# Summing 32768 rows of float32: loads without a cast, one running float32 sum on VectorE, TensorE for the last rows only

## The chip, the cores and the metric

The kernel runs on one core of a Trainium2 chip; the other cores are idle. The metric is the device time of one execution in microseconds (us); lower is better.

## The reference

```python
def setup_inputs():
    batch, seq, dim = 32, 1024, 2048
    return {"grad_output": np.random.randn(batch, seq, dim).astype(np.float32)}

def reference(grad_output):
    return np.sum(grad_output, axis=(0, 1)).astype(np.float32)
```

There are 32768 rows of 2048 numbers, 268.4 MB, to be read, and 8 KB to be written. In this text "a row" of work is a block of 128 rows, one per partition (1.05 MB in memory). There are 256 of them.

## The kernel before

The input is loaded in tiles of eight such rows, 8.39 MB each. The requests are issued by GpSimd, and the transfer casts to float16 on the way. VectorE adds the two halves of a tile, which leaves 8192 columns, and TensorE multiplies these with a column of ones, which sums over the partitions. The sums of all tiles accumulate in four PSUM banks.

```python
PRE_TILES = 2                 # two float32 rows first, on the sync queue
BULK_M = 8
BULK_TAPER = (4, 2)
TAIL_TILES = 5                # five single rows, then one row in four column pieces
T_BUFS = 3
TAIL_BUFS = 8
BULK_ENGS = ("gpsimd",)
# ... [plan: 2 float32 rows; 30 tiles of 8; 2, 4, 2, 1,1,1,1,1 rows; 4 pieces] ...

    for i, entry in enumerate(plan):
        # ... [T is a float16 tile from one of the pools] ...
        getattr(nc, eng_name).dma_start(out=T[:], in_=src)
        red = T
        if uses_dve(entry):
            half = (m * col_n) // 2
            C = c_pool.tile([P, half], fp16, tag="C", name=f"c{i}")
            nc.vector.tensor_tensor(out=C[:], in0=T[:, :half], in1=T[:, half:],
                                    op=mybir.AluOpType.add)
            red = C
        w = ones16 if dt_ is fp16 else ones32        # [128, 1] of ones
        for j in range(n_chunks(entry)):
            nc.tensor.matmul(accs[b][:, :], lhsT=w[:],
                             rhs=red[:, j * MM_N : (j + 1) * MM_N],
                             start=(not started[b]), stop=(n_mm[b] == total_mm[b]))
    # ... [four copies out of PSUM, two on ScalarE and two on VectorE; one store] ...
```

## Time and profile before

| | before |
|---|---|
| median time | 629.0 us (628.98 to 629.04, 3 runs) |
| span of the profiled run | 627.2 us |
| memory read | 268.4 MB, 428 GB/s over the span |
| busy: TensorE, VectorE | 31%, 22% |
| share of the 16 DMA engines used by GpSimd's queue | 98.9% |

The page of the kernel before begins with the busy time of each engine. The row called DMA gives the busy tenths of the 16 DMA engines in 40 slices of the span. The line of a queue (q0 is GpSimd's, q1 the sync queue's) gives its packets, the MB that it wrote (half of those read, because of the cast) and its share of the engines.

```profile
PE 195.1 (31%) x536; PEld 58.1 (9%) x536; DVE 138.9 (22%) x37; ACT 2.4 (0%) x3; POOL 22.6 (4%) x46
...
DMA  9999999999999999999999999999999999999997
...
q0 software_dynamic: 6048, 133.17, 98.9%
q1 hardware_dynamic: 290, 2.11, 0.9%
...
HBM read 268.44 MB, written 0.01 MB: 428 GB/s over the span
```

Nothing but the transfers is busy throughout. The next lines are VectorE's timeline: start, duration, what it did, and in brackets how long it was idle before and what ended the wait.

```profile
27.41 4.42 DVE L152 TENSOR_TENSOR c<-t 128x8192 f16<-128x8192 f16 x1 [26.51 <-DMA t<-in_grad_output_dram]
46.74 4.43 DVE L152 TENSOR_TENSOR c<-t 128x8192 f16<-128x8192 f16 x1 [14.90 <-DMA t<-in_grad_output_dram]
66.06 4.43 DVE L152 TENSOR_TENSOR c<-t 128x8192 f16<-128x8192 f16 x1 [14.90 <-DMA t<-in_grad_output_dram]
...
588.89 4.42 DVE L152 TENSOR_TENSOR c<-t 128x8192 f16<-128x8192 f16 x1 [14.94 <-DMA t<-in_grad_output_dram]
```

The additions start 19.3 us apart, although one takes only 4.4 us, and each waits for a transfer. A tile of 8.39 MB in 19.32 us is 434 GB/s of reading. What an engine does inside these 19.3 us costs nothing as long as it fits.

The end of the span, on all engines:

```profile
620.52 3.57 PE L161 MATMUL psum<-t,ones 128*1 128x512 f16 x8 [0.96 <-DMA t<-in_grad_output_dram]
...
622.85 0.57 ACT L175 COPY res<-psum 1x512 f32<-1x512 f32 x1 [620.82 <-PE psum L161]
...
624.13 0.68 DVE L177 COPY res<-psum 1x512 f32<-1x512 f32 x1 [0.17 <-PE psum L161]
624.90 0.32 SPq L178 DMA_DIRECT2D out_dram<-res  x1
```

At 620.52 us the last single row has arrived and TensorE starts eight matmuls without a gap. Four belong to this row and four to the last row, which comes in four pieces.

### The profile page before, as it was taken

The numbers are of one execution on the slowest core, as the hardware profiler recorded it, in microseconds if no ns is written. First come the engines' busy times: TensorE is split into PE (matmuls) and PEld (weight loads), VectorE is DVE, ScalarE is ACT, GpSimd is POOL, SyncE is SP. The second block draws the span as 40 slices with busy tenths as digits, with TensorE's granted clock in tenths as the row PEclk, the third lists the DMA queues.
The fourth block names the chain that finished last, engine by engine and source line by source line (L and its number), as shares of the span: only waits on it lengthen the run. The fifth ranks groups of instructions, "written<-read, shape, count | busy, mean of one in ns | idle before, by whom it ended". The sixth has DMA issues, their size and how long they took to land.

```text
span 627.2 us, 1267 instructions
## 1 busy us (share of the span) xinstructions
PE 195.1 (31%) x536; PEld 58.1 (9%) x536; DVE 138.9 (22%) x37; ACT 2.4 (0%) x3; POOL 22.6 (4%) x46
## 2 busy tenths in 40 slices
PE   3323320333203333123341134321333312343165
PEld 0001100011000111001110011100111000111011
DVE  0202222022220122211222202222022221122320
ACT  0000000000000000000000000000000000000000
POOL 1000000000000000000000000000000000000110
PEclk9677556775567665667655776656676567665677
DMA  9999999999999999999999999999999999999997
GB/s 242 226 234 201 234 201 234 202 232 203 232 203 232 203 232 203 232 204 230 205 230 205 230 205 230 205 230 206 228 207 228 207 224 211 224 211 221 206 206 139
DMA packets 6344, 135.36 MB, mean 216 GB/s; under 512 B 705, under 2 KB 1217, under 8 KB 1857
## 3 DMA queue, kind: packets, MB, share of 16 engines
q0 software_dynamic: 6048, 133.17, 98.9%
q1 hardware_dynamic: 290, 2.11, 0.9%
q8 instruction: 4, 0.07, 0.0%
q14 instruction: 2, 0.02, 0.0%
HBM read 268.44 MB, written 0.01 MB: 428 GB/s over the span
## 4 chain that ended last, share of the span: by engine, by line
another core or an unknown queue 66%; DVE 21%; DMA 11%; PE 1%; POOL 1%; issue 0%; DVEq 0%; POOLq 0%
DVE c L152 20%; DMA t<-in_grad_output_dram 11%; PE psum L161 1%; POOL t L146 1%; DVEq L152 0%; DVE res L177 0%; POOLq L193 0%
## 5 line engine op out<-in xcount | busy, mean ns | idle before, releaser
L161 PE MATMUL psum<-c,ones 128*1 128x512 f16 x496 | 175.9, 533 | 405.5 <-DVE c L152 405.5
L152 DVE TENSOR_TENSOR c<-t 128x8192 f16<-128x8192 f16 (+2 forms) x33 | 137.5, 4167 | 471.1 <-DMA t<-in_grad_output_dram 471.1
L161 PEld LDWEIGHTS <-ones 128*1 128x1 f16 x520 | 56.5, 109 | 537.5 <-issue 516.4
L146 POOL DMA_DIRECT2D t<-in_grad_output_dram x42 | 22.4, 538 | 590.4 <-DVE c L152 575.3
L161 PE MATMUL psum<-t,ones 128*1 128x512 f16 (+1 forms) x40 | 19.4, 639 | 23.5 <-DMA t<-in_grad_output_dram 23.5
L177 DVE COPY res<-psum 1x512 f32<-1x512 f32 x2 | 1.4, 679 | 13.9 <-PE psum L161 13.9
L161 PEld LDWEIGHTS psum<-t,ones 128*1 128x1 f32 x16 | 1.6, 106 | 27.5 <-DMA t<-in_grad_output_dram 14.1
L175 ACT COPY res<-psum 1x512 f32<-1x512 f32 x2 | 1.1, 575 | 621.1 <-PE psum L161 621.1
L175 ACT ACT_TABLE_LOAD x1 | 1.3, 1283 | 0.7 <-PEq L193 0.7
L104 DVE MEMSET ones<- 128x1 f16 x1 | 0.1, 59 | 0.8 <-PEq L193 0.8
L193 POOL MEMSET const-float32-0.0<- 128x1 f32 x1 | 0.1, 100 | 0.2 <-issue 0.2
L193 POOL MEMSET const-bfloat16-1.0<- 128x1 bf16 x1 | 0.1, 103 | 0.0
L193 POOL MEMSET const-float32-1.0<- 128x1 f32 x1 | 0.1, 100 | 0.0
L193 POOL MEMSET const-uint8-127<- 128x1 uint8 x1 | 0.1, 100 | 0.0
L108 DVE MEMSET ones<- 128x1 f32 x1 | 0.1, 59 | 0.0
## 6 DMA issues: line engine op xcount, KB each, us to landing
t<-in_grad_output_dram POOLq DMA_DIRECT2D x30, 4096.0 KB, 53.1
t<-in_grad_output_dram POOLq DMA_DIRECT2D x5, 512.0 KB, 20.4
t<-in_grad_output_dram SPq DMA_DIRECT2D x2, 1024.0 KB, 14.3
t<-in_grad_output_dram POOLq DMA_DIRECT2D x2, 1024.0 KB, 26.6
t<-in_grad_output_dram POOLq DMA_DIRECT2D x1, 2048.0 KB, 29.0
t<-in_grad_output_dram POOLq DMA_DIRECT2D x4, 128.0 KB, 16.1
out_dram<-res SPq DMA_DIRECT2D x1, 8.0 KB
```

Source lines behind the costliest of these rows:

```text
L104: nc.vector.memset(ones16[:], 1.0)
L108: nc.vector.memset(ones32[:], 1.0)
L146: getattr(nc, eng_name).dma_start(out=T[:], in_=src)
L152: nc.vector.tensor_tensor(out=C[:], in0=T[:, :half], in1=T[:, half:], op=mybir.AluOpType.add)
L161: nc.tensor.matmul(accs[b][:, :], lhsT=w[:], rhs=red[:, j * MM_N : (j + 1) * MM_N], start=(not started[b]), stop=(n_mm[b] == total_mm[b]),)
L175: nc.scalar.copy(out=dst, in_=accs[b][:, :])
L177: nc.vector.tensor_copy(out=dst, in_=accs[b][:, :])
L193: nc = _bacc.Bacc("TRN2", target_bir_lowering=False, num_devices=1)
```

## The change

The intent is to drop the cast, to let the sync queue issue the loads, to keep one float32 sum of 128x2048 on VectorE in place of pair sums in float16, and to use TensorE only for the last rows. There it works in four column groups, each with 32 columns of ones and its own quarter of the partitions of PSUM. The diff, cut to its core:

```diff
-BULK_ENGS = ("gpsimd",)
+ROWS = 8
+GROUPS = 4
+SPLIT = 4
+TAIL = (4, 2, 1)
+PE_ROWS_LAST = 5
 ...
+    ones = const_pool.tile([P, 32], fp32)
+    acc = const_pool.tile([P, D], fp32)
+    head = psum_pool.tile([P, (SPLIT - 1) * C], fp32)     # C = 128 columns
+    last = psum_pool.tile([P, C], fp32)
 ...
+    def sum_row(src):
+        v = src.rearrange("p (k g i) -> p k g i", k=SPLIT, g=GROUPS)
+        for g in range(GROUPS):
+            q = slice(32 * g, 32 * g + 32)
+            mm(head[q, :].rearrange("p (k i) -> p k i", i=C), ("h", g), v[:, : SPLIT - 1, g, :], False)
+        for g in range(GROUPS):
+            q = slice(32 * g, 32 * g + 32)
+            mm(last[q, :], ("l", g), v[:, SPLIT - 1, g, :], False)
 ...
-        getattr(nc, eng_name).dma_start(out=T[:], in_=src)           # float16 tile
-            nc.vector.tensor_tensor(out=C[:], in0=T[:, :half], in1=T[:, half:], ...)
+    for t in range(n_bulk):                                          # 31 tiles of 8 rows
+        T = io_pool.tile([P, ROWS * D], fp32, tag="T", name=f"t{t}")
+        nc.sync.dma_start(out=T[:], in_=src)
+        on_pe = PE_ROWS_LAST if t == n_bulk - 1 else 0
+        for j in range(ROWS):
+            part = T[:, j * D : (j + 1) * D]
+            if j >= ROWS - on_pe:
+                sum_row(part)
 ...
+            else:
+                nc.vector.tensor_add(out=acc[:], in0=acc[:], in1=part)
+    T = io_pool.tile([P, ROWS * D], fp32, tag="T", name="tail")
+    for i, m in enumerate(TAIL):                                     # 4, 2, 1 rows
+        nc.sync.dma_start(out=T[:, at * D : (at + m) * D], in_=src)
+        ... sum_row of each row ...
+        if i == 0:
+            sum_row(acc[:])
+    for k in range(SPLIT):                                           # last row, four pieces
+        nc.sync.dma_start(out=dst, in_=flat[row : row + P, k * W : (k + 1) * W])
+        ... four matmuls, one per column group ...
+    nc.scalar.copy(out=res[:, :n], in_=head[:])
+    nc.vector.tensor_copy(out=res[:, n:], in_=last[:])
+    ... two stores ...
```

More of the change, by code (lines that the diff above doesn't have):

```diff
@@ L9 @@
 P = 128
-MM_N = 512
-PRE_TILES = 2
-PRE_M = 1
-PRE_ENGS = ("sync", "sync")
-BULK_M = 8
-BULK_TAPER = (4, 2)
-USE_DVE = True
-TAIL_TILES = 5
-COL_SPLIT_LAST = True
-T_BUFS = 3
-C_BUFS = 3
-TAIL_BUFS = 8
-BULK_ENGS = ("gpsimd",)
-OUT_COPY_ENGS = ("scalar", "vector")
+ROWS = 8
[3 more added lines that the diff above has]
+PE_ROWS_LAST = 5
 @with_exitstack
@@ L35 @@
     fp32 = mybir.dt.float32
-    fp16 = mybir.dt.float16
     D = out.shape[-1]
@@ L40 @@
     R = flat.shape[0]
-    assert R % P == 0 and D % MM_N == 0
-    nbanks = D // MM_N
-    n_row_blocks = R // P
-    pre_tiles = min(PRE_TILES, n_row_blocks // PRE_M // 4)
-    col_split = COL_SPLIT_LAST and nbanks > 1
-    taper = [m for m in BULK_TAPER if m < BULK_M]
-    n_small = TAIL_TILES + (1 if col_split else 0)
-    while pre_tiles * PRE_M + sum(taper) + n_small > n_row_blocks:
-        if TAIL_TILES and n_small > 1:
-            n_small -= 1
-        elif taper:
-            taper = taper[1:]
-        else:
-            col_split = False
-            n_small = min(n_small, 1)
-            break
@@ L58 @@
-    n_tail = n_small - (1 if col_split else 0)
-    plan: list = []
-    row = 0
-    for i in range(pre_tiles):
-        plan.append((row, PRE_M, fp32, PRE_ENGS[i % len(PRE_ENGS)], 0, D))
-        row += P * PRE_M
-    tail_start = R - P * (n_small + sum(taper))
-    bi = 0
-    while row < tail_start:
-        take = min(P * BULK_M, tail_start - row)
-        plan.append((row, take // P, fp16, BULK_ENGS[bi % len(BULK_ENGS)], 0, D))
-        bi += 1
-        row += take
-    for m in taper:
-        plan.append((row, m, fp16, BULK_ENGS[bi % len(BULK_ENGS)], 0, D))
-        bi += 1
-        row += P * m
@@ L76 @@
-    for _ in range(n_tail):
-        plan.append((row, 1, fp16, BULK_ENGS[bi % len(BULK_ENGS)], 0, D))
-        bi += 1
-        row += P
-    if col_split:
-        for b in range(nbanks - 1, -1, -1):
-            plan.append((row, 1, fp16, BULK_ENGS[bi % len(BULK_ENGS)], b * MM_N, MM_N))
-            bi += 1
-        row += P
-    assert row == R
-    io_pool = ctx.enter_context(tc.tile_pool(name="io", bufs=T_BUFS))
-    pre_pool = None
-    if pre_tiles:
-        pre_pool = ctx.enter_context(tc.tile_pool(name="pre", bufs=pre_tiles))
@@ L91 @@
-    c_pool = None
-    if USE_DVE:
-        c_pool = ctx.enter_context(tc.tile_pool(name="csum", bufs=C_BUFS))
-    n_small_tiles = n_tail + (nbanks if col_split else 0)
-    tail_pool = None
-    if n_small_tiles:
-        tail_pool = ctx.enter_context(
-            tc.tile_pool(name="tail", bufs=min(n_small_tiles, TAIL_BUFS))
-        )
+    W = D // SPLIT
+    C = W // GROUPS
+    n_bulk = (R // P - sum(TAIL) - 1) // ROWS
+    assert (n_bulk * ROWS + sum(TAIL) + 1) * P == R
+    io_pool = ctx.enter_context(tc.tile_pool(name="io", bufs=3))
@@ L100 @@
     const_pool = ctx.enter_context(tc.tile_pool(name="const", bufs=1))
     psum_pool = ctx.enter_context(tc.tile_pool(name="psum", bufs=1, space=bass.MemoryType.PSUM))
-    ones16 = const_pool.tile([P, 1], fp16)
-    nc.vector.memset(ones16[:], 1.0)
-    ones32 = None
-    if pre_tiles:
-        ones32 = const_pool.tile([P, 1], fp32)
-        nc.vector.memset(ones32[:], 1.0)
-    accs = [
-        psum_pool.tile([1, MM_N], fp32, tag=f"psum{b}", name=f"psum{b}")
-        for b in range(nbanks)
-    ]
@@ L114 @@
-    res = const_pool.tile([1, D], fp32)
-    def uses_dve(entry) -> bool:
-        _, m, dt_, _, _, col_n = entry
-        return USE_DVE and dt_ is fp16 and m > 1 and col_n == D
-    def n_chunks(entry) -> int:
-        _, m, dt_, _, _, col_n = entry
-        n = (m * col_n) // MM_N
-        return n // 2 if uses_dve(entry) else n
-    total_mm = [0] * nbanks
-    for e in plan:
-        for j in range(n_chunks(e)):
-            total_mm[((e[4] + j * MM_N) % D) // MM_N] += 1
-    started = [False] * nbanks
@@ L130 @@
-    n_mm = [0] * nbanks
-    for i, entry in enumerate(plan):
-        row0, m, dt_, eng_name, col_lo, col_n = entry
-        rows = flat[row0 : row0 + m * P]
-        if col_n == D:
-            src = rows.rearrange("(p m) d -> p (m d)", p=P)
-        else:
-            src = rows[:, col_lo : col_lo + col_n]
-        if dt_ is fp16:
-            big = m > 1 and col_n == D
-            pool, tag = (io_pool, "T") if big else (tail_pool, "Ttail")
-            T = pool.tile([P, m * col_n], fp16, tag=tag, name=f"t{i}")
-        else:
-            T = pre_pool.tile([P, m * col_n], fp32, tag="Tpre", name=f"t{i}")
-        getattr(nc, eng_name).dma_start(out=T[:], in_=src)
-        red = T
-        if uses_dve(entry):
-            half = (m * col_n) // 2
-            C = c_pool.tile([P, half], fp16, tag="C", name=f"c{i}")
-            nc.vector.tensor_tensor(
-                out=C[:], in0=T[:, :half], in1=T[:, half:], op=mybir.AluOpType.add
-            )
-            red = C
-        w = ones16 if dt_ is fp16 else ones32
-        for j in range(n_chunks(entry)):
-            b = ((col_lo + j * MM_N) % D) // MM_N
-            n_mm[b] += 1
-            nc.tensor.matmul(
-                accs[b][:, :],
-                lhsT=w[:],
-                rhs=red[:, j * MM_N : (j + 1) * MM_N],
-                start=(not started[b]),
-                stop=(n_mm[b] == total_mm[b]),
-            )
-            started[b] = True
@@ L170 @@
-    bank_order = list(range(nbanks - 1, -1, -1)) if col_split else list(range(nbanks))
-    for k, b in enumerate(bank_order):
-        eng = OUT_COPY_ENGS[k % len(OUT_COPY_ENGS)]
-        dst = res[:, b * MM_N : (b + 1) * MM_N]
-        if eng == "scalar":
-            nc.scalar.copy(out=dst, in_=accs[b][:, :])
-        else:
-            nc.vector.tensor_copy(out=dst, in_=accs[b][:, :])
-    nc.sync.dma_start(out=out[None, :], in_=res[:])
+    ones = const_pool.tile([P, 32], fp32)
+    nc.vector.memset(ones[:], 1.0)
@@ new lines, with mm @@
+    acc = const_pool.tile([P, D], fp32)
+    head = psum_pool.tile([P, (SPLIT - 1) * C], fp32)
+    last = psum_pool.tile([P, C], fp32)
+    res = const_pool.tile([P, SPLIT * C], fp32)
+    started = set()
+    def mm(dst, g, src, stop):
+        nc.tensor.matmul(
+            dst, lhsT=ones[:], rhs=src, start=(g not in started), stop=stop,
+            skip_group_check=True,
+        )
+        started.add(g)
+    def sum_row(src):
[6 more added lines that the diff above has]
+            mm(last[q, :], ("l", g), v[:, SPLIT - 1, g, :], False)
@@ new lines @@
+    row = 0
+    for t in range(n_bulk):
+        T = io_pool.tile([P, ROWS * D], fp32, tag="T", name=f"t{t}")
+        src = flat[row : row + P * ROWS].rearrange("(p m) d -> p (m d)", p=P)
+        nc.sync.dma_start(out=T[:], in_=src)
+        row += P * ROWS
+        on_pe = PE_ROWS_LAST if t == n_bulk - 1 else 0
[3 more added lines that the diff above has]
+                sum_row(part)
+            elif t == 0 and j == 0:
+                continue
+            elif t == 0 and j == 1:
+                nc.vector.tensor_add(out=acc[:], in0=T[:, :D], in1=part)
+            else:
+                nc.vector.tensor_add(out=acc[:], in0=acc[:], in1=part)
@@ new lines @@
+    T = io_pool.tile([P, ROWS * D], fp32, tag="T", name="tail")
+    at = 0
+    for i, m in enumerate(TAIL):
+        src = flat[row : row + P * m].rearrange("(p m) d -> p (m d)", p=P)
+        nc.sync.dma_start(out=T[:, at * D : (at + m) * D], in_=src)
+        row += P * m
+        for j in range(m):
+            sum_row(T[:, (at + j) * D : (at + j + 1) * D])
+        at += m
+        if i == 0:
+            sum_row(acc[:])
+    for k in range(SPLIT):
+        dst = T[:, at * D + k * W : at * D + (k + 1) * W]
+        nc.sync.dma_start(out=dst, in_=flat[row : row + P, k * W : (k + 1) * W])
+        for g in range(GROUPS):
+            q = slice(32 * g, 32 * g + 32)
+            into = head[q, k * C : (k + 1) * C] if k < SPLIT - 1 else last[q, :]
+            mm(into, ("h" if k < SPLIT - 1 else "l", g), dst[:, g * C : (g + 1) * C], k >= SPLIT - 2)
@@ L182 @@
+    o = out.rearrange("(k g i) -> g k i", k=SPLIT, g=GROUPS)
+    n = (SPLIT - 1) * C
+    nc.scalar.copy(out=res[:, :n], in_=head[:])
+    nc.vector.tensor_copy(out=res[:, n:], in_=last[:])
+    rows = res[:].rearrange("(g r) c -> g r c", r=32)[:, 0, :]
+    nc.scalar.dma_start(
+        out=o[:, : SPLIT - 1, :], in_=rows[:, :n].rearrange("g (k i) -> g k i", i=C)
+    )
+    nc.sync.dma_start(out=o[:, SPLIT - 1, :], in_=rows[:, n:])
 _INS = ['grad_output']
```

## The prediction

> **What bounds the kernel now.** The transfers from memory. The page shows the 16 DMA engines at nine tenths or more in 39 of 40 slices, the GpSimd-issued queue alone at 98.9% of the span, and TensorE 31% and VectorE 22% busy. The timeline of VectorE shows one big addition (a tile of 8 rows per partition, 8.39 MB in memory) every 19.3 us: 4.4 us of work, then 14.9 us idle, ended each time by a DMA. 8.39 MB in 19.32 us is 434 GB/s of reading. Of the rest, about 3 us pass before data flows at full rate, and the last data land near 620.5 us; then come 8 queued matmuls (3.6 us), two copies (each engine) and the store, to 627.2 us. The measured time is 1.8 us over the span.
>
> **What changes.**
> 1. Transfers. The same 268.4 MB are read, but uncast, and so 268 MB instead of 134 MB are written to the on-chip memory; issue goes from GpSimd to the sync queue. The Trainium skill, "DMA: Bandwidth & Descriptors" (Where 436 GB/s comes from), gives 435 GB/s as the ceiling of the 16 ports. This trace already reads at 434, so I take the engines to be limited by the stream they read; halving the written bytes bought the old kernel nothing, and doubling them should cost little. 31.997 tiles' worth at 19.32 us are 618 us. Up to 1% lost for both sides at their ceiling would add 6 us.
> 2. VectorE. 242 float32 additions of 128x2048 replace 33 additions in float16. The skill, "VectorE: DVE Perf Modes" (perf-mode tier table), gives one float32 element per cycle, 2293 ns for 2048; the trace has no such addition, but its float16 one of 128x4096 took 2293 ns, twice the elements at twice the rate. Estimate: 8 x 2.29 = 18.3 us a tile, perhaps 18.8 with gaps between dependent additions, against 19.3 us of transfer. So VectorE goes from 22% to about 90% busy and stays just ahead; 5 of the last bulk tile's 8 rows go to TensorE, so that nothing piles up.
> 3. TensorE. 536 matmuls vanish except for 14 rows at the end. A float32 128x512 matmul pair took 0.85 us twice at the cold clock here; in four column groups side by side I estimate 1.7 us a row cold. That keeps up with rows arriving every 2.4 us. All of this was off the critical path.
> 4. Ends. Tail transfers are all requested about 20 us ahead (no waits for small buffers, which the DMA share of 0.85 in the last 27 us hints at), and after the last quarter only four small matmuls and one copy remain: about 2 us saved. The start is nearly unchanged.
>
> **Sum.** About 2.5 to 3 us start + 618 to 621 us stream + 4 us end + 1.8 us: 627.5 us. Large parts of the work are removed, but from engines that were waiting. Range 620 to 638. Chances: faster by over 2%: 0.04; within 2%: 0.87; slower: 0.09.
>
> **What would show it.** Step 1: landings of 8 MB tiles about 19.3 us apart, 425 to 434 GB/s written, DMA share still near 1. Step 2: additions of 2.29 us, about eight tenths to nine tenths of VectorE, each first one of a tile waiting for a DMA by about 0.5 to 1 us. Step 4: under 5 us between the last landing and the end.
>
> **What would make it wrong.** Additions over 2.41 us start to start: then VectorE bounds, each further 0.1 us costing 24 us. A plain float32 stream on the sync queue below 425 GB/s: each 1% costs 6 us. Or a stream above 434, if the cast or GpSimd's descriptors, not the ports, set the present rate.

## More of the kernel before

The columns are: stretch in us, its length, busy time of TensorE, weight loads, VectorE, ScalarE and GpSimd (with the number of instructions), granted clock, DMA share, and GB/s written.

```profile
621.00:621.50 0.50, 0.50 (x3) 0.15 (x2) 0.00 (x0) 0.00 (x0) 0.00 (x0) 0.50 1.22 201
...
622.00:622.50 0.50, 0.50 (x2) 0.13 (x1) 0.00 (x0) 0.00 (x0) 0.00 (x0) 0.50 0.38 61
622.50:623.00 0.50, 0.50 (x2) 0.13 (x1) 0.00 (x0) 0.15 (x1) 0.00 (x0) 0.50 0.10 14
623.00:623.50 0.50, 0.50 (x3) 0.13 (x1) 0.23 (x1) 0.42 (x1) 0.00 (x0) 0.50 0.00 0
```

Data moved until about 622.9 us. The pieces landed while TensorE still had a backlog, and so no wait for them is recorded.

## The result

| | before | after |
|---|---|---|
| median time, same rounds | 629.02 us (4 runs) | 630.18 us (4 runs) |
| span of the profiled run | 627.2 us | 628.6 us |
| ratio of the times | | 1.0019, 95% interval 1.0005 to 1.0033 |
| busy: TensorE, VectorE | 31%, 22% | 3%, 88% |
| bytes written by transfers | 135.4 MB | 268.5 MB |

A ratio here is the mean time of one kernel's fast runs over the mean of the other's fast runs of the same rounds, and so it is not quite the ratio of the medians. The two kernels differ by 0.2%, inside the 2% that counts as the same. The predicted time was 627.5 us and the range 620 to 638 us.

The page after the change:

```profile
PE 16.2 (3%) x240; PEld 7.9 (1%) x240; DVE 555.0 (88%) x244; ACT 1.8 (0%) x2; POOL 0.2 (0%) x4
...
DMA  9999999999999999999999999999999999999996
...
q1 hardware_dynamic: 5480, 268.44, 98.9%
...
HBM read 268.44 MB, written 0.01 MB: 427 GB/s over the span
```

The written bytes have doubled and the queue is another one, and the DMA engines are nearly as full as before: 98.9%, against 99.8% for the two queues of the kernel before (98.9% and 0.9%). VectorE's timeline, where a line stands for the eight additions of a tile:

```profile
22.71 2.29 DVE L79 TENSOR_TENSOR acc<-t 128x2048 f32<-128x2048 f32 x1 [21.82 <-DMA t<-in_grad_output_dram]
25.04 13.92 DVE L81 TENSOR_TENSOR acc<-acc,t 128x2048 f32<-128x2048 f32 x6
42.12 18.58 DVE L81 TENSOR_TENSOR acc<-acc,t 128x2048 f32<-128x2048 f32 x8 [3.16 <-DMA t<-in_grad_output_dram]
61.47 18.57 DVE L81 TENSOR_TENSOR acc<-acc,t 128x2048 f32<-128x2048 f32 x8 [0.78 <-DMA t<-in_grad_output_dram]
...
139.03 18.57 DVE L81 TENSOR_TENSOR acc<-acc,t 128x2048 f32<-128x2048 f32 x8 [0.92 <-DMA t<-in_grad_output_dram]
159.30 18.57 DVE L81 TENSOR_TENSOR acc<-acc,t 128x2048 f32<-128x2048 f32 x8 [1.70 <-DMA t<-in_grad_output_dram]
...
430.57 18.57 DVE L81 TENSOR_TENSOR acc<-acc,t 128x2048 f32<-128x2048 f32 x8 [1.14 <-DMA t<-in_grad_output_dram]
450.52 18.57 DVE L81 TENSOR_TENSOR acc<-acc,t 128x2048 f32<-128x2048 f32 x8 [1.37 <-DMA t<-in_grad_output_dram]
...
585.96 18.57 DVE L81 TENSOR_TENSOR acc<-acc,t 128x2048 f32<-128x2048 f32 x8 [0.77 <-DMA t<-in_grad_output_dram]
605.31 6.95 DVE L81 TENSOR_TENSOR acc<-acc,t 128x2048 f32<-128x2048 f32 x3 [0.78 <-DMA t<-in_grad_output_dram]
```

A tile now lands every 19.35 us (333.46 minus 314.11 us, and most other pairs of the same view). Its eight additions take 18.57 us, and VectorE then waits about 0.78 us for the next tile. So it stays ahead of the transfers by 4% of its time. Four waits are longer without a reason in the program: 0.92 us before 139.03, 1.70 us before 159.30, 1.14 us before 430.57 and 1.37 us before 450.52. (The 3.16 us before 42.12 are there because the first tile has one addition fewer.)

The end on all engines:

```profile
605.35 1.50 PE L50 MATMUL head<-t,ones 128*32 128x384 f32 x8 [605.35 <-DMA t<-in_grad_output_dram]
...
607.03 1.53 PE L50 MATMUL head<-t,ones 128*32 128x384 f32 x8
...
611.53 0.83 PE L50 MATMUL head<-t,ones 128*32 128x384 f32 x8
...
622.38 0.85 PE L50 MATMUL head<-tail,ones 128*32 128x384 f32 x8 [0.53 <-DMA tail<-in_grad_output_dram]
...
624.94 0.43 PE L50 MATMUL last<-tail,ones 128*32 128x128 f32 x8 [0.20 <-DMA tail<-in_grad_output_dram]
...
625.44 0.29 DVE L106 COPY res<-last 128x128 f32<-128x128 f32 x1 [13.18 <-PE last L50]
625.75 0.66 SPq L111 DMA_DIRECT2D out_dram<-res  x1
```

The rows on TensorE start 1.7 us apart at first (605.35, 607.03) and 0.86 us apart later. They keep up with the data. The last piece lands just before 624.94 us; four pairs of small matmuls, a copy of 0.29 us and the store follow, and the span ends at 628.6 us.

### The profile page after: what moved, and what is told of

The parts are those of the page before. It is cut to its first block, busy times and chain, and to the rows that moved or that the text cites. A ratio compares the mean times of both kernels' runs of the same rounds, so it can differ in the third digit from the quotient of the medians.

```text
span 628.6 us, 874 instructions
## 1 busy us (share of the span) xinstructions
PE 16.2 (3%) x240; PEld 7.9 (1%) x240; DVE 555.0 (88%) x244; ACT 1.8 (0%) x2; POOL 0.2 (0%) x4
## 3 DMA queue, kind: packets, MB, share of 16 engines
q1 hardware_dynamic: 5480, 268.44, 98.9%
## 4 chain that ended last, share of the span: by engine, by line
DMA 69%; DVE 29%; issue 0%; SPq 0%; PE 0%; DVEq 0%
DMA t<-in_grad_output_dram 63%; DVE acc L81 29%; DMA tail<-in_grad_output_dram 6%; SPq L97 0%; SPq L87 0%; PE last L50 0%; SPq L69 0%; DVE res L106 0%; DVEq L81 0%
## 5 line engine op out<-in xcount | busy, mean ns | idle before, releaser
L81 DVE TENSOR_TENSOR acc<-acc,t 128x2048 f32<-128x2048 f32 x241 | 552.4, 2292 | 34.9 <-DMA t<-in_grad_output_dram 27.7
L50 PE MATMUL head<-t,ones 128*32 128x384 f32 x40 | 6.5, 723 | 605.4 <-DMA t<-in_grad_output_dram 605.4
L79 DVE TENSOR_TENSOR acc<-t 128x2048 f32<-128x2048 f32 x1 | 2.3, 2291 | 21.8 <-DMA t<-in_grad_output_dram 21.8
L50 PEld LDWEIGHTS head<-t,ones 128*32 128x32 f32 x40 | 1.8, 156 | 605.3 <-DVE acc L81 605.3
L50 PE MATMUL head<-tail,ones 128*32 128x384 f32 (+1 forms) x80 | 7.1, 428 | 3.6 <-DMA tail<-in_grad_output_dram 3.6
L50 PE MATMUL last<-tail,ones 128*32 128x128 f32 x64 | 3.2, 274 | 0.2 <-DMA tail<-in_grad_output_dram 0.2
L50 PE MATMUL last<-t,ones 128*32 128x128 f32 x40 | 2.9, 362 | 0.0
L50 PEld LDWEIGHTS head<-tail,ones 128*32 128x32 f32 x80 | 2.0, 109 | 4.9 <-DMA tail<-in_grad_output_dram 4.9
L50 PEld LDWEIGHTS last<-tail,ones 128*32 128x32 f32 x64 | 2.0, 110 | 3.2 <-issue 2.7
L50 PEld LDWEIGHTS last<-t,ones 128*32 128x32 f32 x40 | 1.9, 150 | 3.4 <-issue 3.4
```

The costliest lines, as they stand in the source:

```text
L50: nc.tensor.matmul(dst, lhsT=ones[:], rhs=src, start=(g not in started), stop=stop, skip_group_check=True,)
L79: nc.vector.tensor_add(out=acc[:], in0=T[:, :D], in1=part)
L81: nc.vector.tensor_add(out=acc[:], in0=acc[:], in1=part)
```

## The experiments

The theory: both kernels move at the pace of the 16 DMA engines, and the few tenths of a percent between them come from the stream and its two ends. The rivals: VectorE at 88% slows the stream; the sync queue is a slower source; the doubled writes cost more than they seem to. There were ten experiments and one repetition of the new kernel.

### e1_one_add: one addition in eight (wrong result)

```diff
             elif t == 0 and j == 0:
                 continue
+            elif j > 1 or (t > 0 and j > 0):
+                continue
```

> Wrong result on purpose: one of eight additions per tile is kept. If the transfers alone set the pace (my theory): 629 to 631 us, tiles still landing 19.35 us apart, VectorE about 11% busy. If the nearly full VectorE or the late release of its buffers slows the stream (rival): 4 us less, 626 us, with landings 19.2 to 19.3 us apart.

Measured: 629.9 us, ratio to before 1.0019 (1.0006 to 1.0032), VectorE 11% busy. That is the ratio of the full kernel. Tiles still landed 19.35 us apart. Taking away seven eighths of VectorE's work saves nothing that the ratio shows, so its load is off the critical path and does not set the period of the stream. The rival with its 626 us falls. The single delays did change: here all thirty tiles after the first landed on time, where late tiles cost the new kernel 2 us; but the last eight rows took 1.3 us longer than there. What stays open, below, comes back to this.

### e2_pool_f32: float32 loads issued by GpSimd

```diff
-        nc.sync.dma_start(out=T[:], in_=src)
+        nc.gpsimd.dma_start(out=T[:], in_=src)
```
The other two load lines are changed in the same way.

> The new kernel with its float32 loads issued by GpSimd instead of the sync queue. If the issuing queue does not matter (my theory): 629 to 631 us. If the sync queue is what made the stream end some 2 us later than in the kernel before (rival): 626 to 628 us and the last data as early as before.

Measured: 630.62 us, ratio 1.0032 (1.0020 to 1.0045), correct. The sync queue is not the slower source. If anything the new kernel gained a little by it: the first tile landed at 22.71 us with it and at 23.56 us with GpSimd's queue.

### e3_pool_cast: the same with the cast to float16

```diff
-        T = io_pool.tile([P, ROWS * D], fp32, tag="T", name=f"t{t}")
+        T = io_pool.tile([P, ROWS * D], fp16, tag="T", name=f"t{t}")
```
This is on top of e2. The matmuls of loaded rows use float16 ones; the running sum stays float32.

> The new kernel with GpSimd loads cast to float16, so that half the bytes are written; the sum stays float32 in VectorE. If the written bytes are free (my theory): within 1 us of the run with float32 loads from GpSimd. If doubling them cost the stream 0.5% (rival): 2 to 4 us less than that run, about 626 us, and faster than both kernels, because it has the early stream of the one and the short end of the other. VectorE additions should stay 2.29 us, as one operand is still float32.

Measured: 629.0 us, ratio 1.0002 (0.9989 to 1.0016), correct; 1.6 us less than e2. The timelines of VectorE in the same stretch, first with float32 loads (e2):

```profile
314.51 18.57 DVE L81 TENSOR_TENSOR acc<-acc,t 128x2048 f32<-128x2048 f32 x8 [0.78 <-DMA t<-in_grad_output_dram]
...
391.91 18.58 DVE L81 TENSOR_TENSOR acc<-acc,t 128x2048 f32<-128x2048 f32 x8 [0.78 <-DMA t<-in_grad_output_dram]
```

and with the cast (e3):

```profile
314.31 18.58 DVE L84 TENSOR_TENSOR acc<-acc,t 128x2048 f32<-128x2048 f32 x8 [0.75 <-DMA t<-in_grad_output_dram]
...
391.61 18.58 DVE L84 TENSOR_TENSOR acc<-acc,t 128x2048 f32<-128x2048 f32 x8 [0.75 <-DMA t<-in_grad_output_dram]
```

Four tiles took 77.40 us in e2 and 77.30 us in e3: 19.35 against 19.325 us a tile. Over 32 tiles that is 0.8 us. So the written bytes are nearly free, but not quite: halving them is worth 0.13% of the stream. The whole difference between the two medians is 1.6 us, so the theory's own number, within 1 us, was missed too. 0.8 us are in the period; in the two profiled runs, which are 1.3 us apart, another 0.2 us are in single delays and 0.1 us each in the start and in what follows the last big tile. The rival that doubled writes cost 0.5% falls, and so does its 626 us. The additions stayed at 2.29 us although one operand is float16.

### e4_nine_adds: nine additions a tile (wrong result)

```diff
                 nc.vector.tensor_add(out=acc[:], in0=acc[:], in1=part)
+                if j == 1:
+                    nc.vector.tensor_add(out=acc[:], in0=acc[:], in1=part)
```

> Wrong result on purpose: nine additions per tile instead of eight. Nine at 2.32 us start to start are 20.9 us against 19.35 us of transfer, so VectorE becomes the bound: about 666 us (42 + 29 x 20.9 + 9 for the last additions + about 9 for the end and the offset). If a second limit hides behind the transfers, more; if VectorE has more room than the trace suggests, 631 us.

Measured: 670.95 us, ratio 1.067. VectorE's timeline, where the extra addition has a line of its own (L83):

```profile
48.98 18.57 DVE L81 TENSOR_TENSOR acc<-acc,t 128x2048 f32<-128x2048 f32 x8
67.59 2.29 DVE L83 TENSOR_TENSOR acc<-acc,t 128x2048 f32<-128x2048 f32 x1
69.92 18.57 DVE L81 TENSOR_TENSOR acc<-acc,t 128x2048 f32<-128x2048 f32 x8
```

A tile now takes 20.93 us (69.92 minus 48.98) and no wait is left: VectorE is the bound. The last addition ended at 658.34 us; the terms of the expectation give 657.1 us. Most of the missing 5 us are at the end. The running sum stands ahead of the last four rows in TensorE's order, TensorE was slow after its idle time (1.7 us a row), and so 10.8 us passed from there to the end of the span. One ninth addition turns a free engine into the bound, which shows how narrow the room of 0.78 us is.

### e5_no_groups: the last rows without column groups

```diff
-    head = psum_pool.tile([P, (SPLIT - 1) * C], fp32)
-    last = psum_pool.tile([P, C], fp32)
+    accs = [psum_pool.tile([1, W], fp32, tag=f"acc{k}", name=f"acc{k}") for k in range(SPLIT)]
 ...
+            accs[k][:, :], lhsT=ones[:, :1], rhs=src, start=(k not in started), stop=stop,
 ...
+        for k in range(SPLIT):
+            mm(k, src[:, k * W : (k + 1) * W], False)
```
The copies out of PSUM (four) and the store (one) change with it.

> The new kernel, but its last rows are summed by plain matmuls of 128x512 with one column of ones, one after the other. Worked out from the durations of the kernel before (0.43 us for each of the two halves of a float32 matmul at the full clock, twice that cold): 3.4 us a row at the full clock, 14 rows in a row from 605.3 us, the first 5 us at half speed, so TensorE ends near 656 us and the run takes about 661 us. If the column groups are only decoration (rival): 630 to 632 us.

Measured: 660.04 us, ratio 1.0499, correct. Its chain of work that ended last (start, length, what):

```profile
565.16 39.37 DMA t<-in_grad_output_dram
...
604.66 50.08 PE acc L48 x112
...
654.77 0.68 DVE tail L97
```

TensorE works for 50 us without a break after the last big tile has landed. Four rows took 13.90 us at the full rate, 3.47 us a row, against 0.86 us in the new kernel: four groups side by side are four times as fast. The Trainium skill, "TensorEngine Tiling (Array Packing)", section Theoretical Speedup, gives up to 4x for a dimension of at most 32, and the trace reaches it. Without the groups, float32 matmuls would not fit behind rows that come every 2.4 us.

### e6_all_vector: no row of the last big tile on TensorE

```diff
-PE_ROWS_LAST = 5
+PE_ROWS_LAST = 0
```

> No row of the last big tile goes to TensorE, so VectorE adds all eight and ends 18.6 us after that tile landed, near 624 us; the running sum and the last four rows are then multiplied on a cold TensorE. About 636 us. If the five rows on TensorE bring nothing (rival): 630 us.

Measured: 635.33 us, ratio 1.0101, correct. VectorE finished at 623.5 us and TensorE started the running sum then, with three rows and the pieces behind it. Handing five rows over is worth 5 us at the end, which is where an engine that is otherwise free comes onto the path.

### e7_nine_small: the kernel before with nine small buffers

```diff
-TAIL_BUFS = 8
+TAIL_BUFS = 9
```

> The kernel before with nine small buffers instead of eight, so that no request at its end waits for a buffer. My prediction took such waits to cost part of 2 us: then 627 us. If the requests were early enough anyway and the transfers stay busy (what the trace of after now suggests, rival): within 0.3 us of the kernel before, about 628.8 us.

Measured: 628.94 us, ratio 1.0003 (0.9989 to 1.0017), correct. The wait for a small buffer, which the prediction suspected, cost nothing that the time shows. Only the last request had it: it goes out at 611.34 us, where it went at 612.72 us in the kernel before. The two requests in front of it wait 6.26 and 4.35 us for a transfer to land, with nine buffers as with eight; those waits are not tested.

### e8_both: the better pieces together

```diff
+    for t in range(2):
+        F = const_pool.tile([P, D], fp32, name=f"pre{t}")
+        nc.sync.dma_start(out=F[:], in_=flat[row : row + P])
 ...
+    bulk = [ROWS] * ((R // P - 2 - sum(TAIL) - 1) // ROWS)        # 30 tiles of 8 rows
+    bulk.append(R // P - 2 - sum(TAIL) - 1 - sum(bulk))           # and one of 6, all on TensorE
```
This is on top of e3.

> The pieces that came out best: two float32 rows on the sync queue first (early start), all else cast to float16 from GpSimd (19.32 instead of 19.35 us a tile), float32 running sum on VectorE, column groups at the end. If the remaining differences are start, period and end as read from the traces: 0.9 us less than the run with cast loads, about 628.0 us, just under both kernels. If these differences are scatter: 629 us or more.

Measured: 634.79 us, ratio 1.0096, correct: a miss. GpSimd's timeline of its requests near the end:

```profile
568.77 0.53 POOL L78 DMA_DIRECT2D t<-in_grad_output_dram  x1 [18.80 <-DVE acc L85]
606.07 1.58 POOL L91 DMA_DIRECT2D tail<-in_grad_output_dram  x3 [36.77 <-PE last L50]
```

and the DMA engines in these stretches (columns as above):

```profile
598.00:602.00 4.00, 0.00 (x0) 0.00 (x0) 3.97 (x2) 0.00 (x0) 0.00 (x0) 1.00 0.83 178
602.00:605.00 3.00, 1.99 (x37) 1.29 (x40) 2.93 (x3) 0.00 (x0) 0.00 (x0) 1.00 0.01 3
```

The request for the last rows waited until TensorE was done with the tile of six rows, and the compiled program has this wait, where the one of e3 has a wait for VectorE's earlier tile. Presumably the last rows had been given the buffer of the tile of six. From 602 to 605 us the DMA engines were idle, for lack of a request.

### e9_own_tail: a buffer of its own for the last rows

```diff
-    T = io_pool.tile([P, ROWS * D], fp16, tag="T", name="tail")
+    T = const_pool.tile([P, ROWS * D], fp16, name="tail")
```

> The combined kernel with a buffer of its own for the last rows, so that their request need not wait for TensorE. If that wait was what cost the combined kernel 6 us (its transfers ran dry at 602 to 607 us): 627.5 to 628.3 us, at most 0.2% below the kernel before. If something else in it is slow: about 634 us again.

Measured: 634.78 us, ratio 1.0097, correct: a miss too, for another reason. The view of the line that requests the last rows gives the first and last start of these requests:

```profile
L91 POOL DMA_DIRECT2D tail<-in_grad_output_dram x3: 547/547/547, 46.9 to 85.5; - x3
```

and two lines of the end, of VectorE and of TensorE:

```profile
608.83 18.57 DVE L85 TENSOR_TENSOR acc<-acc,t 128x2048 f32<-128x2048 f32 x8 [0.75 <-DMA t<-in_grad_output_dram]
623.30 0.51 PE L50 MATMUL head<-t,ones 128*32 128x384 f16 x4 [623.30 <-DMA t<-in_grad_output_dram]
```

With nothing to wait for, the requests were moved to 46.9 to 85.5 us. So the last data to land were those of a tile of eight rows for VectorE (608.83 us) and the tile of six (623.30 us). VectorE ended at 627.4 us and all fourteen rows of TensorE came after 623.3 us. What has to come last for the sake of the end was loaded first. The wait of e8 is therefore not tested alone by this run: it removed the gap and made a new end.

### e10_after_again: the new kernel once more

> The new kernel unchanged, beside the combined one on the same chip: 630 us, 1.001 to 1.003 of the kernel before, as in its first measurement.

Measured: 630.2 us, ratio 1.0021 (1.0008 to 1.0033). The difference of 0.2% is there again.

### e11_first_sync: the cast version with its first tile on the sync queue

```diff
+        if t == 0:
+            T = const_pool.tile([P, ROWS * D], fp32, name="t0")
+            nc.sync.dma_start(out=T[:], in_=src)
+        else:
             T = io_pool.tile([P, ROWS * D], fp16, tag="T", name=f"t{t}")
             nc.gpsimd.dma_start(out=T[:], in_=src)
```
This is on top of e3.

> The cast version, but with its first tile in float32 from the sync queue, which starts 0.7 us before GpSimd's queue; the end is left as it was in the cast version. If the start is what the cast version lacked: 628.1 to 628.4 us, 0.1% below the kernel before. If the last few tenths are scatter: 629.0 us, the same as the kernel before. The combined kernels at 634.8 us lost their time at the end (a request that waited for TensorE, or requests moved ahead), which does not occur here.

Measured: 628.28 us against 629.08 us for the kernel before, ratio 0.9989 (0.9975 to 1.0002), correct. This is the best version, and its interval still touches 1, so it is not shown to beat the kernel before. VectorE's timeline has a surprise:

```profile
39.72 2.29 DVE L86 TENSOR_TENSOR acc<-t 128x2048 f32<-128x2048 f32 x1 [38.78 <-DMA t<-in_grad_output_dram]
42.05 367.46 DVE L88 TENSOR_TENSOR acc<-acc,t 128x2048 f32<-128x2048 f32 x158
410.00 18.58 DVE L88 TENSOR_TENSOR acc<-acc,t 128x2048 f32<-128x2048 f32 x8 [0.48 <-DMA t<-in_grad_output_dram]
```

The first tile landed at 39.72 us, 16 us later than in e3. It shared the DMA engines with the first requests of the other queue. The Trainium skill, "DMA: Bandwidth & Descriptors", section Queues, rings and completion order, says that an engine takes turns between its queues packet by packet; this landing at twice the time of a tile agrees with it. VectorE then worked for 367 us without a wait and had caught up at 410 us. Its room of about 0.78 us a tile paid the 16 us back, and the late landing cost nothing, because bytes arrive in whatever order at the same rate.

## Why the prediction was right or wrong, point by point

- **The bound.** The prediction said that the removed work belonged to engines that were waiting, and that the time would stay within 2%. It did (1.0019). e1 shows it for the work added to VectorE: with and without it the ratio is 1.0019. Inside the 2% the direction was wrong: 627.5 us is 1.5 us below the kernel before, and the new kernel came out 1.2 us above it. The gain that one might expect from dropping nearly all matmuls and the cast was never to be had, because none of it was on the path.
- **Step 1, the stream: right in kind, small in size.** The prediction quoted the skill's ceiling of 435 GB/s ("DMA: Bandwidth & Descriptors", Where 436 GB/s comes from). The traces show 434.2 GB/s with the cast (8.389 MB in 19.32 us) and 433.5 GB/s without it (in 19.35 us), so the case agrees with that figure of the page. It does not show the reason that the page gives, the ports on the chip's side: with the cast only 217 GB/s were written there, and the reading was no faster than 434 GB/s. Nor does the remark in the same section hold here that the memory side, at about 358 GB/s, binds transfers from memory. What on the reading side sets the rate, no run tells. "Doubling them should cost little" is right; e2 and e3 put it at 0.025 us a tile.
- **Step 2, VectorE.** The addition took 2.292 us, against the 2.293 us that the prediction quoted. Eight took 18.57 us, between the predicted 18.3 and 18.8, and the wait of 0.78 us lies within the predicted 0.5 to 1 us. e4 shows that the warning about 2.41 us was in place: with 20.93 us a tile, the time is 671 us.
- **Step 3, TensorE.** 1.7 us a row was right while it was slow, and e5 shows that the column groups make it so.
- **Step 4, the ends: the saving was over-sized.** "About 2 us saved" failed. The prediction took 620.5 us for the landing of the last data; it was the last recorded wait, and data moved until about 622.9 us behind a backlog of matmuls. From the arrival of the last single row to the end of the span, the kernel before took 6.7 us (627.2 minus 620.52) and the new one 6.2 us (628.6 minus 622.38), so 0.5 us was saved. The end term of the sum itself, 4 us after the last landing, held: it was 3.7 us. The suspected wait for a small buffer cost nothing (e7).
- **The sum.** The span of the new kernel can be added up from its timeline: 3.36 us before the stream is at its rate (22.71 minus one period of 19.35), 19.35 us for the first tile, 582.6 us for the next thirty (605.31 minus 22.71), 19.63 us for the last eight rows (624.94 minus 605.31) and 3.7 us to the end, in all 628.6 us. The mis-sized term is the stream: 621.6 us, where the prediction had 618 to 621. It counted whole periods at 19.32 us and no delays; there were 2.1 us of delays (582.6 minus 30 periods of 19.35 us). The start was 3.4 us instead of 2.5 to 3. These two make up most of the 2.7 us between 627.5 and 630.2. (The span is that of the slowest of the four runs, 630.5 us, and the prediction's own terms add up to 626.3 to 629.8 us, so 627.5 lay in their lower half.)
- **Why the new kernel is slower by 0.2% at all.** The same reckoning for the kernel before gives 3.3 us and a stream of about 619.8 us: 24.15 us for its first ten rows, 561.48 us for 29 tiles (588.89 minus 27.41), and 34.2 us for the last fourteen rows, to the completion mark of the last transfer in the trace, at 623.08 us. That leaves 4.1 us for its end. The new stream is thus 1.8 us longer: 0.8 us by the period (32 times 0.025) and 1.0 us by single delays (2.1 against 1.1). The shorter end, 3.7 instead of 4.1 us, gives 0.4 us back. What is left is the 1.4 us between the spans. Of this only the part of the period was tested by itself (e2 against e3).

What stays open: the single delays. In the trace's list of packets, a queue that the page calls "instruction" moved 8 KB packets at about 143 and 434 us in the new kernel. By the completion marks of the transfers (the trace records when each one signals that it has landed), the next tiles to land, at 159.21 and 450.43 us, were 0.9 and 1.0 us late; no other big tile was late by more than 0.15 us. (The tile added from 430.57 us had landed on time, at 430.11 us; there VectorE itself was late.) The delays are not scatter: e10 and e2 have packets and late tiles at the same places, late by 0.6 to 0.95 us. e1, whose VectorE program is an eighth as long, has no such packet between its start and 607 us and no late tile; the rows that landed next after 607 us were 0.8 us late. That fits a fetch of instructions that takes DMA time. Against it stand packets with no late tile behind them: one at about 572 us in e2, one at about 147 us in e8, and in the kernel before three of four packets of 16 KB of this kind, at about 268, 425 and 577 us (the one at 113 us goes with a clear delay, the pair of tiles at 104.81 and 125.10 us, 20.3 us apart). So it is argued from coincidence, not shown.

## What to carry to other kernels

When one resource is full from end to end, work that moves between the other engines changes nothing until one of them fills too; compute the room left per tile before and after (here it fell from 14.9 us to 0.78 us), because it is the next limit. A wait that is not recorded is not proof that the data were there early: an engine with a backlog hides it, and the DMA activity by stretches tells when data really ended. At the end of a stream the order counts: what lands last should need the least work, and a request moved earlier or tied to another buffer can cost more than all the tuning of the middle (5 to 6 us in e6, e8 and e9, against 1 us for the stream).

## What the Trainium skill lacked or had wrong

- "DMA: Bandwidth & Descriptors" gives 435 GB/s as the ceiling of the ports on the chip's side, but does not say that a load that casts is held to the same rate by the bytes it reads: 434.2 GB/s read with 217 GB/s written, 433.5 GB/s read with as much written.
- "TensorE: Matmul & The Clock Gate", Part 1, says that an idle TensorE falls to half rate and needs about 3.4 us of work to recover, and warns that the recorded clock events are unreliable. The first holds roughly: after 605 us of idling the float32 matmuls of 128x384 took 847 ns at first and 486 ns later, and the change came 5.5 us after the first matmul (605.35 to 610.88 us); in e10 it came after 2.9 us. The warning is not borne out here: the trace's first clock record, at 610.88 us, stands where the durations change. The view by stretches reads 1.00 from 604 to 614 us all the same, because it shows 1.00 wherever no record stands, so the durations have to be read beside it.
- "VectorE: DVE Perf Modes" describes a pipeline flush after each operation of roughly the operation's duration less 266 ns, and says that an operation that is not held starts earlier. Dependent additions of 2.292 us started 2.326 us apart here: the gap seen is 0.034 us, where the flush by that rule would be about 2.0 us (an estimate from the page).
- No page says how little a tile's late landing matters: 16 us in e11 were made up over 370 us.
